# Hybrid attention and RWKV-7 block on one core: the state's decay on GpSimd, its sum on VectorE, and the group norm of 512 tokens before the scan's end

## The chip, the core and the metric

The kernel runs on one core of one Trainium2 chip, as one launch. The metric is the device time of that launch in microseconds. The engines are named as the profile names them: PE is TensorE (PEld its weight loads), DVE is VectorE, ACT is ScalarE, POOL is GpSimd, SP is SyncE, whose queue issues all DMAs of this kernel.

## The reference

One layer of a diffusion backbone over 2048 latent tokens of width 1024, with 256 context tokens ahead of them. All data are fp32. The latent tokens go through an RMS norm, one wide projection, two mixer branches, a merge, and a squared-ReLU MLP. Branch A is windowed attention. Branch B is an RWKV-7 scan in both directions, 8 heads of 64 channels:

```python
def step(S, inp):
    r_t, w_t, kk_t, b_t, k_t, v_t = inp
    sa = jnp.einsum('bhvk,bhk->bhv', S, -kk_t)
    S = S * w_t[:, :, None, :] + sa[..., None] * b_t[:, :, None, :] + v_t[..., None] * k_t[:, :, None, :]
    y = jnp.einsum('bhvk,bhk->bhv', S, r_t) if emit else None
...
mu = jnp.mean(y, axis=-1, keepdims=True)
var = jnp.mean(jnp.square(y - mu), axis=-1, keepdims=True)
yn = (y - mu) * lax.rsqrt(var + LNX_EPS)
...
out = (yn.reshape(B, L, RWKV_WIDTH) * lnx_w + lnx_b + bonus.reshape(B, L, RWKV_WIDTH)).astype(hg.dtype)
g = jax.nn.sigmoid(hg) @ gate_g2
return out * g
...
x = x + gate1 * ((ga * (ya @ w_branch_attn) + gr * (yr @ w_branch_rwkv)) @ w_out)
x = x + gate2 * (jnp.square(jax.nn.relu(h @ w_up)) @ w_down)
out = rmsnorm(x, norm_f_g)
```

## The kernel before

The program has four stages. The first (to about 982 us) projects the tokens, computes the second branch's inputs and leaves them in DRAM: `ka_d`, `rho_d`, `v_d`, and `bk_d`, which holds b and k per chunk of 64 tokens. The second runs the scan, and beside it, to fill PE, the attention, sixteen groups of gate projections and the attention branch's projection. The third merges the branches. The fourth is the MLP.

**The scan.** There are 36 steps, each one chunk of 64 tokens in each of the two directions, four chunks to a window, nine windows. The state of a direction lies as `w[r, 1, h]` in the step's tile `w`, 64 x 256 for each half `r` of the partitions. A step has six parts. Part 0 is `chain_g`: state times keys on PE (`ch<-w,kr`), copied by ACT to `g`. Part 1 is `chain_u`: `g` times the chunk's inverse `st` (`ch<-g,st`), copied by ACT into `w`. Part 2 is `chain_s`: PE adds up the new state in PSUM, first the old state through a product with the identity (`ch<-w,ident`, fp32), then b and k, transposed in `bt`, times the chunk's vectors (`ch<-w,bt`); DVE multiplies the sum by the chunk's decay `pc` and writes it as the next step's state (L710). Then follow the chunk's outputs (`ch<-bm,w`, `ch<-kr,w`). Part 3 is `turn`: PE transposes the next step's `bks` (`tb`), ACT copies it to `bt`. Parts 4 and 5 are `before`: the next step's products of b, k with keys and receptances (`gb`), masked by DVE.

**The inverse.** For each window of four steps, ahead of its use, DVE works out the inverses of the chunks' triangular matrices, in an unbroken row of small operations in SBUF (L588, L590) with transposes around them (L582, L599).

**What runs beside.** After each part, `beside` advances the attention (`attend`) twice and the filler (`fill`) once: gate projections of the first 1024 tokens (`gate`, `gt<-gh,gw_hi`; weights split by ACT into `gw_hi` and by POOL into `gw_lo`), then the attention branch of four blocks of 512 tokens (`branch`, `gt<-ya_h,wa_h`, one PSUM bank, read by DVE at L991). The last block needs the last attention output `ya_d`. `mods` loads the remaining modulation weights (`adp<-ada_w,silr`), one piece a step.

**The order on each engine** is not that of the source alone: the tile framework orders each engine's instructions by its own plan of when operands come; only the scan's matmuls (`rpe`) keep their order among themselves. Each engine then runs its list strictly in order.

**The merge.** `rwkv_out(tb)` does the group norm, the bonus and the gate of 512 tokens; the blocks come as 1, 0, 2, 3. `load_branch` brings `w_branch_rwkv`. `merge_weights` makes `gate1` and `gate2` as rows along all partitions (16 products with diagonal tiles `dg`), scales `w_out` by gate1 and splits it into `wo_h`, `wo_l`; it stands after the first block's branch products (`mb`) and before its output products (`mm`).

Of the kernel before, what the change touches and what calls it, by code (L numbers as in the profile page):

```python
# [22 lines left out]
H = 8  # L23
# [24 lines left out]
def tile_hybrid_block(ctx: ExitStack, tc: tile.TileContext, io: dict, out: bass.AP):  # L48
# [15 lines left out]
    ma_d = dram.tile([KC, P, SEQ], F32, name="ma_d")  # L64
    bon_d = dram.tile([NP, P, SEQ], F32, name="bon_d")
# [20 lines left out]
    def col(o, n=1):  # L86
        return pp[:, o:o + n]
# [953 lines left out]

    att, flr = attend(), fill()
# [13 lines left out]

    mods = (x for m in range(4) for x in ada2(m))
# [10 lines left out]
    for i, _ in enumerate(first):  # L1068
        if i == 0:
            for s in cur:  # L1070
                turn(s)
        if 1 <= i < 3:
            before(cur[i - 1])
# [25 lines left out]
    for _ in att:  # L1099
        pass  # L1100
    for _ in flr:
        pass
# [11 lines left out]
    p3 = ExitStack()  # L1114
    mo = p3.enter_context(tc.tile_pool(name="mo", bufs=1, reuse_waits="tile"))
    mw = p3.enter_context(tc.tile_pool(name="mw", bufs=1, reuse_waits="tile"))
    mb = p3.enter_context(tc.tile_pool(name="mb", bufs=2, reuse_waits="tile"))
    mp = p3.enter_context(tc.tile_pool(name="mp", bufs=2, reuse_waits="tile"))
# [20 lines left out]
    def rwkv_out(tb):  # L1139

        t0 = tb * TB
        yT = mp.tile([P, NP, TB], F32, name="yT", bufs=1)
# [56 lines left out]
    wo_h = mo.tile([P, KC, D], F32R, name="wo_h")  # L1199
    wo_l = mo.tile([P, KC, D], F32R, name="wo_l")  # L1200

    def merge_weights():
# [4 lines left out]
        for m, half, dst in ((0, 0.5, gate1), (3, 1.0, (gate2[:, 0:512], gate2[:, 512:D]))):  # L1207
# [8 lines left out]

        w_out = io["w_out"].rearrange("(k p) n -> p k n", p=P)
        for k in range(KC):
# [5 lines left out]
            act.activation(wo_h[:, k], raw, AF.Copy)  # L1224
            (pool, dve)[k % 2].tensor_tensor(out=wo_l[:, k], in0=raw, in1=wo_h[:, k].bitcast(F32), op=ALU.subtract)

    blocks = (1, 0, 2, 3)
    br = rwkv_out(blocks[0])
    for at, tb in enumerate(blocks):
# [16 lines left out]
        if at == 0:  # L1246
            merge_weights()
        if at + 1 < len(blocks):
            br = rwkv_out(blocks[at + 1])
        for i in range(TB // P):  # L1250
            x = mw.tile([P, D], F32, name="x1t", bufs=2)
            sp.dma_start(out=x, in_=io["x"][t0 + i * P:t0 + (i + 1) * P])
            for hf in range(2):
                cs = slice(hf * 512, (hf + 1) * 512)
                ps = mps.tile([P, 512], F32, name="mm")
                for k in range(KC):
                    lh, ll = mh[:, k, i * P:(i + 1) * P], ml[:, k, i * P:(i + 1) * P]
                    pe.matmul(ps, lh, wo_h[:, k, cs], start=(k == 0), stop=False)  # L1258
                    pe.matmul(ps, lh, wo_l[:, k, cs], start=False, stop=False)  # L1259
                    pe.matmul(ps, ll, wo_h[:, k, cs], start=False, stop=(k == KC - 1))  # L1260
# [228 lines left out]
```

## Time and profile before

| what | value |
|---|---|
| median of 3 runs | 4223.32 us (4220.43 to 4228.75) |
| the profiled execution's own time | 4228.56 us |
| its span, first to last instruction | 4226.8 us |
| TensorE busy | 3865.3 us, 91% of the span |
| VectorE busy | 2171.9 us, 51% |
| ScalarE busy | 1359.5 us, 32% |
| GpSimd busy | 1349.6 us, 32% |
| mean granted TensorE clock | 0.932 of full speed |
| DMA engines busy in the MLP, from 2800 us on | 0.20 of their time |

The shares are means over four stages that have different limits. A clock of 1.0 is 2.4 GHz, 0.5 is 1.2 GHz; a mean between them says what part of a stretch ran at which. A wait counts only where the engine that sets the pace waits.

### The profile page before, as it was taken

What the parts mean: (1) busy time and instruction counts of PE and PEld (TensorE: products, weight loads), DVE (VectorE), ACT (ScalarE), POOL (GpSimd) and SP (SyncE); (2) the same over time, 40 slices, a digit from 0 to 9 for tenths busy, and PEclk for the clock granted to TensorE, in tenths of its full rate; (3) what the DMA queues carried; (4) which work ended last, traced back from release to release, by engine and by line L of the source; (5) the groups of instructions that cost most, each with busy time, mean ns of one, the idle gap of its engine ahead of it and who ended that gap; (6) DMA issues with size and microseconds to landing.
All of it is one profiled execution on the core that took longest, in us unless ns stands there. A gap on an engine that the chain in (4) does not pass through costs nothing.

```text
span 4226.8 us, 67796 instructions
## 1 busy us (share of the span) xinstructions
PE 3865.3 (91%) x26788; PEld 3148.4 (74%) x26788; DVE 2171.9 (51%) x3794; ACT 1359.5 (32%) x2476; POOL 1349.6 (32%) x1104
## 2 busy tenths in 40 slices
PE   7989978897899989888898779989999999999999
PEld 5778868785677767766676658768888888888887
DVE  3355277767576366556566364444443345444334
ACT  2353444554343333322322233331212213112121
POOL 3353555554221110000000174533433334443231
PEclk8999979897999989797897889999999999999999
DMA  6665566666544445343442545542211214211111
GB/s 236 202 195 158 161 183 188 188 185 184 164 138 138 125 131 148 106 132 96 131 139 83 158 150 179 176 154 65 70 50 40 60 41 130 69 60 60 40 55 45
DMA packets 617587, 529.95 MB, mean 125 GB/s; under 512 B 156212, under 2 KB 536340, under 8 KB 616244
## 3 DMA queue, kind: packets, MB, share of 16 engines
q1 hardware_dynamic: 617268, 525.60, 41.6%
q8 instruction: 211, 3.46, 0.3%
q14 instruction: 108, 0.88, 0.1%
HBM read 381.09 MB, written 144.38 MB: 124 GB/s over the span
## 4 chain that ended last, share of the span: by engine, by line
PE 58%; DVE 6%; DMA 4%; issue 2%; POOL 2%; SPq 1%; ACT 1%; POOLq 0%; DVEq 0%; ACTq 0%
PE fd L1343 5%; PE fd L1344 5%; PE fd L1345 5%; PE fu L235 5%; PE fu L236 5%; PE fu L237 5%; PE ch L535 5%; PE gt L947 3%; PE ops L883 3%; PE gb L535 2%; DVE au L582 1%; PE sc L835 1%; PE mm L1260 1%; PE mm L1258 1%; PE mm L1259 1%
## 5 line engine op out<-in xcount | busy, mean ns | idle before, releaser
L235 PE MATMUL acc<-hh,w_hi 128*128 128x384 f32 (+6 forms) x1304 | 457.4, 353 | 41.6 <-ACT hh L211 18.9
L237 PE MATMUL acc<-hh,w_lo 128*128 128x384 f32 (+6 forms) x1304 | 455.8, 351 | 10.3 <-POOL w_lo L229 10.3
L236 PE MATMUL acc<-hl,w_hi 128*128 128x384 f32 (+6 forms) x1304 | 456.5, 351 | 4.8 <-POOL hl L212 4.8
L1349 DVE TENSOR_TENSOR acc<-fd,acc 128x512 f32<-128x512 f32 x480 | 322.3, 686 | 249.1 <-PE fd L1345 246.8
L235 PE MATMUL fu<-h2h,up_h 128*128 128x512 f32 x1024 | 403.4, 394 | 5.8 <-ACT rl L1330 5.8
L1343 PE MATMUL fd<-dn_h,g_h 128*128 128x512 f32 x1024 | 399.8, 390 | 3.5 <-DVE acc L1347 3.5
L236 PE MATMUL fu<-h2l,up_h 128*128 128x512 f32 x1024 | 402.6, 393 | 0.0
L237 PE MATMUL fu<-h2h,up_l 128*128 128x512 f32 x1024 | 402.0, 393 | 0.0
L1333 DVE TENSOR_TENSOR g_l<-rl,g_h 128x512 fp32r<-128x512 f32 x128 | 150.0, 1173 | 487.4 <-POOL rl L1332 487.4
L1344 PE MATMUL fd<-dn_l,g_h 128*128 128x512 f32 x1024 | 399.7, 390 | 0.0
L1345 PE MATMUL fd<-dn_h,g_l 128*128 128x512 f32 x1024 | 398.3, 390 | 0.0
L235 PEld LDWEIGHTS acc<-hh,w_hi 128*128 128x128 f32 (+2 forms) x1304 | 256.1, 197 | 67.1 <-ACT hh L211 21.8
L1332 POOL TENSOR_TENSOR rl<-rl 128x512 f32<-128x512 f32 x128 | 149.9, 1171 | 469.2 <-ACT g_h L1331 469.1
L229 POOL TENSOR_TENSOR w_lo<-w_raw,w_hi 128x1024 fp32r<-128x1024 f32 (+1 forms) x92 | 232.7, 2532 | 205.9 <-ACT w_hi L228 185.7
L1330 ACT ACTIVATE rl<-fu 128x512 f32<-128x512 f32 x128 | 76.2, 597 | 654.1 <-PE fu L237 644.9
L237 PEld LDWEIGHTS acc<-hh,w_lo 128*128 128x128 f32 (+2 forms) x1304 | 255.7, 196 | 31.4 <-POOL w_lo L229 12.5
L236 PEld LDWEIGHTS acc<-hl,w_hi 128*128 128x128 f32 (+2 forms) x1304 | 256.0, 196 | 25.1 <-POOL hl L212 6.0
L1287 POOL TENSOR_TENSOR dn_l<-raw,dn_h 128x1024 fp32r<-128x1024 f32 x64 | 155.6, 2450 | 275.1 <-ACT dn_h L1286 275.1
L845 DVE TENSOR_REDUCE mm<-sc 128x1 f32<-128x256 f32 (+1 forms) x256 | 119.0, 477 | 237.9 <-PE sc L837 152.2
L235 PEld LDWEIGHTS fu<-h2h,up_h 128*128 128x128 f32 x1024 | 193.1, 189 | 49.3 <-ACT rl L1330 6.0
L1343 PEld LDWEIGHTS fd<-dn_h,g_h 128*128 128x128 f32 x1024 | 192.9, 188 | 44.9 <-DVE acc L1347 4.0
L237 PEld LDWEIGHTS fu<-h2h,up_l 128*128 128x128 f32 x1024 | 192.7, 188 | 43.5
(305 smaller groups left out, 8292.3 us busy)
## 6 DMA issues: line engine op xcount, KB each, us to landing
w_raw<-in_w_in SPq DMA_DIRECT2D x74, 512.0 KB
raw<-in_w_mlp_up SPq DMA_DIRECT2D x64, 512.0 KB
raw<-in_w_mlp_down SPq DMA_DIRECT2D x64, 512.0 KB
bk_d<-bk SPq DMA_DIRECT2D x36, 512.0 KB
w<-v_d SPq DMA_DIRECT2D x144, 128.0 KB
gw_raw<-in_w_in SPq DMA_DIRECT2D x32, 512.0 KB
ada_w<-in_w_ada SPq DMA_DIRECT2D x32, 512.0 KB
gt<-g_d SPq DMA_DIRECT2D x64, 256.0 KB
```

The source lines that it names most:

```text
L229: pool.tensor_tensor(out=lo[:, :, :m], in0=raw[:, :, :m], in1=hi[:, :, :m].bitcast(F32), op=ALU.subtract)
L235: pe.matmul(ps[:m, :n], wh[:, k, :m], hh[:, k, :], start=(k == 0), stop=False)
L236: pe.matmul(ps[:m, :n], wh[:, k, :m], hl[:, k, :], start=False, stop=False)
L237: pe.matmul(ps[:m, :n], wl[:, k, :m], hh[:, k, :], start=False, stop=(k == KC - 1))
L535: return self.link(nc.tensor.matmul(*a, **k))
L1287: eng.tensor_tensor(out=lo, in0=raw, in1=hi.bitcast(F32), op=ALU.subtract)
L1332: pool.tensor_tensor(out=rl, in0=rl, in1=rl, op=ALU.mult)
L1333: dve.tensor_tensor(out=glo[:, j], in0=rl, in1=gh[:, j].bitcast(F32), op=ALU.subtract)
L1343: pe.matmul(ps, lh, dn[j][0][:, cs], start=(j == 0), stop=False)
L1344: pe.matmul(ps, lh, dn[j][1][:, cs], start=False, stop=False)
L1345: pe.matmul(ps, ll, dn[j][0][:, cs], start=False, stop=(j == FG - 1))
L1349: dve.tensor_tensor(out=acc[:, cs], in0=ps, in1=acc[:, cs], op=ALU.add)
```

## The change

Four edits, and the order of some parts.

1. The state is decayed by POOL, ahead of time: after `chain_g` of a step POOL writes `nxt.w[r, 1, h] = s.w[r, 1, h] * pc` (four operations of 64 x 256 a step). The identity product goes. The sum in PSUM holds only the b, k product, and DVE adds it to what POOL wrote.
2. For this b and k must carry the decay too: the new `decay(s)` multiplies `bks` (128 x 512) by `pc` on POOL, after `before` has read it and before `turn` transposes it. So `before` moves to parts 3 and 4 and `turn` to part 5.
3. `early` does the group norm, bonus and gate of tokens 512 to 1023 in the last window, in quarters of 128 tokens, and stores the result in `yw_d`; the merge's first block then only loads and splits it.
4. `merge_weights` stands before the first block's branch products; its gate2 part comes last; `wo_h`, `wo_l` become one tile per eighth, half of them in a pool of their own, and the pool `mp` comes first in its stage. `mods` goes ahead by one or two pieces a step.

```diff
+    def decay(s):
+
+        pool.tensor_tensor(out=s.bk, in0=s.bk, in1=pc[:, s.d, :, s.c:s.c + 1].broadcast_to([P, NP, P]), op=ALU.mult)
...
-            for s in pair:
-                for h, r in enumerate(hh):
-                    rpe.matmul(s.cp[r, 0], ident[r, r], s.w[r, 1, h], start=True, stop=False, skip_group_check=True)
             for s, nxt in zip(pair, nxts):
                 for p in range(NP):
                     for h, r in enumerate(hh):
-                        rpe.matmul(s.cp[r, 0, p], s.bt[:, p, r], s.w[:, 0, h, p], start=False, stop=True,
+                        rpe.matmul(s.cp[r, 0, p], s.bt[:, p, r], s.w[:, 0, h, p], start=True, stop=True,
                                   skip_group_check=True)
                 for h, r in enumerate(hh):
-                    dve.tensor_tensor(out=nxt.w[r, 1, h], in0=s.cp[r, 0],
-                                      in1=pc[r, s.d, :, s.c:s.c + 1].broadcast_to([C, NP, C]), op=ALU.mult)
+                    dve.tensor_tensor(out=nxt.w[r, 1, h], in0=s.cp[r, 0], in1=nxt.w[r, 1, h], op=ALU.add)
...
+    def early():
...
+        for i in range(EBN // P):
...
+            ps = bank(atp, "ey", "at")
+            for p in range(NP):
+                pe.transpose(ps[:, p * P:(p + 1) * P], yT[:, p], ident)
...
+            pool.tensor_tensor(out=s1[:, 1], in0=s1[:, 1], in1=expo[:, :H], op=ALU.pow)
+            pool.tensor_tensor(out=y3c, in0=y3c, in1=s1[:, 1].unsqueeze(2).broadcast_to([P, H, C]), op=ALU.mult)
+            yield
...
+            dve.tensor_tensor(out=yw, in0=gp.rearrange("p (a t) -> p a t", a=NP), in1=yw, op=ALU.mult)
+            sp.dma_start(out=yw_d[:, :, i * P:(i + 1) * P].rearrange("a p t -> p a t"), in_=yw)
...
-                    next(mods, None)
+                    for s, nxt in zip(cur, nxts):
+                        if nxt is not None:
+                            for h, r in enumerate(hh):
+                                pool.tensor_tensor(out=nxt.w[r, 1, h], in0=s.w[r, 1, h],
+                                                   in1=pc[r, s.d, :, s.c:s.c + 1].broadcast_to([C, NP, C]), op=ALU.mult)
+                    for _ in range(1 + step % 2):
+                        next(mods, None)
...
-                elif part == 3 and nxts[0] is not None:
+                elif part < 5 and nxts[0] is not None:
+                    before(nxts[part - 3])
+                    decay(nxts[part - 3])
+                elif part == 5 and nxts[0] is not None:
                     for s in nxts:
                         turn(s)
-                elif part > 3 and nxts[0] is not None:
-                    before(nxts[part - 4])
                 next(ahead_of, None)
+                if w == NWIN - 1:
+                    ey = ey or early()
+                    for _ in range(2 - part % 2):
+                        next(ey, None)
                 beside(TICKS)
...
+        if EB0 <= t0 < EB0 + EBN:
...
+            for p in range(NP):
+                yw = mp.tile([P, TB], F32, name="yw")
+                sp.dma_start(out=yw, in_=yw_d[p, :, t0 - EB0:t0 - EB0 + TB])
+                split(yh[:, p], yl[:, p], yw)
+            return yh, yl
...
     br = rwkv_out(blocks[0])
+    merge_weights()
...
-        if at == 0:
-            merge_weights()
```

How the instructions stand now, at three places. First PE in step 33 of the scan, from the product with the inverse to the chunk's outputs; the two numbered `ch` tiles are the two directions. Before:

```order
L535 MATMUL ch_23656<-g,st 64x64 x8
L535 MATMUL ch_23667<-g,st 64x64 x8
L535 MATMUL ch_23656<-w,ident 64x256 x2
L535 MATMUL ch_23667<-w,ident 64x256 x2
L535 MATMUL ch_23656<-w,bt 64x64 x8
L535 MATMUL ch_23667<-w,bt 64x64 x8
L535 MATMUL ch_23656<-bm,w 64x64 x8
```

The same place of the change:

```order
L538 MATMUL ch_23857<-g,st 64x64 x8
L538 MATMUL ch_23868<-g,st 64x64 x8
L538 MATMUL ch_23857<-w,bt 64x64 x8
L538 MATMUL ch_23868<-w,bt 64x64 x8
L538 MATMUL ch_23857<-bm,w 64x64 x8
```

The four identity products of the step are gone, and nothing has come in their place.

Then PE at the end of the scan, around the last two rows of the last step's outputs (`ch<-bm,w`, `ch<-kr,w`); `gt<-ya...` is the last block of the attention branch, `ops` and `ot` the attention itself. Before:

```order
L990 MATMUL gt<-ya_h,wa_l 128x512
L535 MATMUL ch_24122<-bm,w 64x64 x8
L535 MATMUL ch_24111<-kr,w 64x64 x8
L535 MATMUL ch_24122<-kr,w 64x64 x8
L988 MATMUL gt<-ya_h,wa_h 128x512
L989 MATMUL gt<-ya_l,wa_h 128x512
L990 MATMUL gt<-ya_h,wa_l 128x512
```

The same place of the change:

```order
L886 MATMUL ops<-vtok,pT 128x65 x4
L538 MATMUL ch_24330<-bm,w 64x64 x3
L538 MATMUL ch_24341<-bm,w 64x64 x8
L538 MATMUL ch_24330<-kr,w 64x64 x8
L538 MATMUL ch_24341<-kr,w 64x64 x8
L899 MATMUL ot<-ident,on 128x128 x4
L1291 MATMUL mt<-dg,ones 128x128 x8
L991 MATMUL gt<-ya_h,wa_h 128x512
L992 MATMUL gt<-ya_l,wa_h 128x512
L993 MATMUL gt<-ya_h,wa_l 128x512
```

Before, the last attention block ended with step 32, and the 96 products of the branch's last block stood between and behind the chain's last steps. Now the attention's last products stand between the chain's last steps, and all 96 branch products follow the scan in one row, with the first `mb` right behind them.

Last POOL late in the scan, where it had only memsets (`st`, `pack`) and the branch's splits (`ya_l`) to do. Before:

```order
L595 MEMSET st 32x32x32 x2
L826 MEMSET pack 128x64 x2
L595 MEMSET st 32x32x32 x2
L826 MEMSET pack 128x64
L979 TENSOR_TENSOR ya_l<-raw,ya_h 128x512 x4
```

The same stretch of the change:

```order
L1143 TENSOR_TENSOR w<-w,pc 64x256 x4
L664 TENSOR_TENSOR bks<-bks,pc 128x512 x2
L829 MEMSET pack 128x64
L598 MEMSET st 32x32x32 x2
L1143 TENSOR_TENSOR w<-w,pc 64x256 x2
L664 TENSOR_TENSOR bks<-bks,pc 128x512
L1143 TENSOR_TENSOR w<-w,pc 64x256 x2
L664 TENSOR_TENSOR bks<-bks,pc 128x512
```

Each step now has four decays of the state (`w`) and two of b and k (`bks`) in POOL's list.

## Rows read from the trace of the kernel before

**Rows 1.** Page, part 1: busy time, share of the span, instructions.

```profile
PE 3865.3 (91%) x26788; PEld 3148.4 (74%) x26788; DVE 2171.9 (51%) x3794; ACT 1359.5 (32%) x2476; POOL 1349.6 (32%) x1104
```

**Rows 2.** Stretches: length; busy of PE, PEld, DVE, ACT, POOL; clock, DMA share, GB/s.

```profile
1124.00:1526.00 402.00, 385.31 (x4146) 299.32 (x4144) 225.96 (x486) 149.10 (x276) 66.68 (x40) 0.98 0.47 131
1526.00:1880.00 354.00, 311.21 (x3966) 246.96 (x3964) 204.30 (x429) 118.70 (x232) 26.55 (x26) 0.87 0.45 132
1880.00:2344.00 464.00, 402.44 (x5120) 318.85 (x5116) 272.36 (x609) 138.72 (x271) 9.71 (x12) 0.86 0.39 113
2344.00:2420.00 76.00, 61.05 (x645) 45.83 (x641) 19.98 (x46) 13.05 (x28) 7.95 (x8) 0.87 0.55 164
2420.00:2475.00 55.00, 40.72 (x173) 28.21 (x172) 31.97 (x55) 15.43 (x25) 40.45 (x35) 0.88 0.50 148
2475.00:2520.00 45.00, 31.67 (x90) 19.13 (x91) 36.44 (x39) 17.06 (x22) 36.92 (x24) 0.66 0.57 169
2520.00:2800.00 280.00, 271.13 (x1223) 215.56 (x1223) 126.82 (x197) 93.10 (x167) 129.16 (x123) 0.98 0.54 175
2800.00:4226.80 1426.80, 1404.47 (x6126) 1152.22 (x6124) 605.19 (x740) 314.37 (x432) 509.44 (x302) 0.99 0.20 63
```

**Rows 3.** Groups by line: busy us, mean ns of one, idle before.

```profile
L535 PE MATMUL ch<-w,ident 64*64 64x256 f32 x280 | 49.0, 440 | 11.9 <-ACT w L695 11.5
L710 DVE TENSOR_TENSOR w<-ch,pc 64x256 f32<-64x256 f32 x140 | 58.9, 421 | 51.2 <-PE ch L535 38.0 <-issue 6.8 <-ACT pT L880 2.4
```

**Rows 4.** PE in order of time in one step, clock full: start, length us.

```profile
2301.72 1.08 PE L535 MATMUL ch<-w,ident 64*64 64x256 f32 x8
2302.73 0.80 PE L535 MATMUL ch<-w,bt 128*64 128x64 f32 x18
```

**Rows 5.** PE's waits, 1124 to 2345 us: us in total, times, longest.

```profile
PE sT L873 <- DVE mm L845: 26.3, 11, 5.9
PE sc L835 <- DVE qA L815: 11.9, 3, 6.1
```

**Rows 6.** Two lines of POOL: ns of one, min/median/max.

```profile
L1161 POOL TENSOR_TENSOR yc<-yc,s x16: 1031/1044/1544, 2421.6 to 2658.1; 128x512 f32<-128x512 f32 x16
L463 POOL TENSOR_TENSOR ks<-ks,ta x32: 721/901/4893, 343.9 to 1052.8; 128x256 f32<-128x256 f32 x32
```

**Rows 7.** DVE and POOL in order of time, during an inverse.

```profile
1353.35 2.62 POOL L929 TENSOR_TENSOR gw_lo<-gw_raw,gw_hi 128x1024 fp32r<-128x1024 f32 x1 [0.88 <-ACT gw_hi L928]
1353.75 2.46 DVE L590 TENSOR_TENSOR tn<-tn,itmp 128x220 f32<-128x220 f32 x1
```

**Rows 8.** Groups by line: the inverse's row on DVE, all nine windows.

```profile
L590 DVE TENSOR_TENSOR tn<-tn,itmp 128x31 f32<-128x31 f32 (+15 forms) x279 | 106.9, 383 | 6.5
L588 DVE TENSOR_TENSOR itmp<-tn,au 128x31 f32<-128x31 f32 (+15 forms) x279 | 97.9, 351 | 6.9
```

**Rows 9.** PE in order of time at the scan's end; [idle before it].

```profile
2342.57 0.66 PE L896 MATMUL ot<-ident,on 128*128 128x128 f32 x4
...
2351.81 1.09 PE L538 MATMUL tb<-ident,bks 128*128 128x128 f32 x8
2357.34 0.68 PE L988 MATMUL gt<-ya_h,wa_h 128*128 128x512 f32 x1 [4.43 <-ACT ya_h L978]
...
2401.72 0.50 PE L988 MATMUL gt<-ya_h,wa_h 128*128 128x512 f32 x1 [0.89 <-DVE gt L991]
...
2410.44 0.79 PE L988 MATMUL gt<-ya_h,wa_h 128*128 128x512 f32 x1 [5.67 <-DVE gt L991]
```

**Rows 10.** The chain of waits from 2340 to 2540 us: start, length.

```profile
2405.50 3.74 DMA yo<-y_d
...
2419.66 0.69 DVE gt L991
...
2439.05 0.70 PE mb L1240 x2
...
2501.99 3.47 DVE x1t L1223 x2
...
2506.59 0.79 PE mm L1258
```

More of the change, by code (lines that the diff above doesn't have):

```diff
@@ L1040, in fill, with load @@
             yield from branch(brp, raw_of, wa, t)
+    def early():
+        wk = [ip.tile([P, 4, NP, P], F32, name="yw0", tag="ga", bufs=1), ip.tile([P, 4, NP, P], F32, name="yw1", tag="st")]
+        aw = ip.tile([P, 1024], F32, name="g2e", tag="au", bufs=1)
+        sg = ip.tile([P, 2, P], F32, name="sge", tag="itmp", bufs=1)
+        g2 = aw[0:96, 0:512]
+        sp.dma_start(out=g2, in_=io["gate_g2"])
+        def load(i):
+            t0 = EB0 + i * P
+            for j in range(P // C):
+                sp.dma_start(out=wk[i % 2][:, 0, :, j * C:(j + 1) * C], in_=y_d[t0 // C + j])
+            sp.dma_start(out=sg[0:96, i % 2], in_=sg_d[:, t0:t0 + P])
+            sp.dma_start(out=wk[i % 2][:, 3], in_=bon_d[:, :, t0:t0 + P].rearrange("a p t -> p a t"))
+        load(0)
+        for i in range(EBN // P):
+            yT, yc, yw, bt = (wk[i % 2][:, j] for j in range(4))
+            s1 = aw[:, 512 + i % 2 * 2 * H:512 + (i % 2 + 1) * 2 * H].rearrange("p (b h) -> p b h", h=H)
+            if i + 1 < EBN // P:
+                load(i + 1)
+            ps = bank(atp, "ey", "at")
+            for p in range(NP):
+                pe.transpose(ps[:, p * P:(p + 1) * P], yT[:, p], ident)
+            y3 = ps.rearrange("p (h c) -> p h c", c=C)
+            dve.tensor_reduce(out=s1[:, 0], in_=y3, axis=AX.X, op=ALU.add)
+            dve.tensor_scalar(out=s1[:, 0], in0=s1[:, 0], scalar1=-1.0 / C, scalar2=None, op0=ALU.mult)
+            ycf = yc.rearrange("p a b -> p (a b)")
+            y3c = ycf.rearrange("p (h c) -> p h c", c=C)
+            dve.tensor_tensor(out=y3c, in0=y3, in1=s1[:, 0].unsqueeze(2).broadcast_to([P, H, C]), op=ALU.add)
+            act.activation(yw, yc, AF.Square)
+            dve.tensor_reduce(out=s1[:, 1], in_=yw.rearrange("p a b -> p (a b)").rearrange("p (h c) -> p h c", c=C),
+                              axis=AX.X, op=ALU.add)
+            pool.tensor_scalar(out=s1[:, 1], in0=s1[:, 1], scalar1=1.0 / C, scalar2=1e-5 * C, op0=ALU.mult, op1=ALU.add)
+            pool.tensor_tensor(out=s1[:, 1], in0=s1[:, 1], in1=expo[:, :H], op=ALU.pow)
+            pool.tensor_tensor(out=y3c, in0=y3c, in1=s1[:, 1].unsqueeze(2).broadcast_to([P, H, C]), op=ALU.mult)
+            yield
+            ps = bank(atp, "eb", "at")
+            for p in range(NP):
+                pe.transpose(ps[:, p * P:(p + 1) * P], yc[:, p], ident)
+            for p in range(NP):
+                act.activation(yw[:, p], ps[:, p * P:(p + 1) * P], AF.Identity, scale=col(O_LW + p), bias=col(O_LB + p))
+            pool.tensor_tensor(out=yw, in0=yw, in1=bt, op=ALU.add)
+            yield
+            gp = bank(atp, "eg", "at")
+            for p in range(NP):
+                pe.matmul(gp[:, p * P:(p + 1) * P], g2[:, p * P:(p + 1) * P], sg[0:96, i % 2], start=True, stop=True)
+            dve.tensor_tensor(out=yw, in0=gp.rearrange("p (a t) -> p a t", a=NP), in1=yw, op=ALU.mult)
+            sp.dma_start(out=yw_d[:, :, i * P:(i + 1) * P].rearrange("a p t -> p a t"), in_=yw)
+            yield
@@ L1068, in tile_hybrid_block @@
     for i, _ in enumerate(first):
-        if i == 0:
+        if i < 2:
+            before(cur[i])
+            decay(cur[i])
+        elif i == 2:
             for s in cur:
                 turn(s)
-        if 1 <= i < 3:
-            before(cur[i - 1])
         beside(1)
@@ L1098, in tile_hybrid_block @@
             pass
[L1099 to L1102, printed above, removed]
+    for it in (ey, att, flr):
+        for _ in it:
+            pass
     p2.close()
@@ L1197, in second_norm @@
             sp.dma_start(out=h2_d[i, :, kh * 4:kh * 4 + 4], in_=hf)
-    wo_h = mo.tile([P, KC, D], F32R, name="wo_h")
-    wo_l = mo.tile([P, KC, D], F32R, name="wo_l")
+    wo_h = [(mv if k < KC // 2 else mo).tile([P, D], F32R, name=f"wo_h{k}") for k in range(KC)]
+    wo_l = [(mv if k < KC // 2 else mo).tile([P, D], F32R, name=f"wo_l{k}") for k in range(KC)]
     def merge_weights():
@@ L1206, in merge_weights, with along @@
         gate1 = [mw.tile([P, 512], F32, name="gate1", tag="wt", bufs=2) for hf in range(2)]
-        for m, half, dst in ((0, 0.5, gate1), (3, 1.0, (gate2[:, 0:512], gate2[:, 512:D]))):
+        def along(m, half, dst):
             for hf in range(2):
```

21 lines of the change are left out of this document (15 added, 6 removed).

## The prediction

> **What bounds the kernel now.** I read the page's busy shares first. PE is busy for 91% of the span, DVE for 51%, ACT and POOL for 32% each [rows 1]. So the question at each place is whether PE itself sets the pace or waits.
>
> The stretches answer it by stage [rows 2]. The MLP from 2800 us on keeps PE busy for 1404.47 of 1426.8 us at a clock of 0.99; the change doesn't touch it. In the scan, from 1124 to 2344 us, PE is busy for 385.31 + 311.21 + 402.44 = 1099 of 1220 us, which is 90%. The 121 us without work are short waits of several kinds, most of them on DVE; the two largest sums are 26.3 and 11.9 us, both of the attention [rows 5]. No wait on the chain of states stands among these two. So the scan is mostly paced by the number of matmuls in PE's list, and the reader should see that work taken off PE there is worth about its own time.
>
> The seam between scan and merge is different. From 2344 to 2520 us PE has idle 14.95 + 14.28 + 13.33 = 42.6 us, and its clock is 0.87, 0.88 and 0.66 [rows 2]. A mean clock of 0.66 says that 68% of the stretch ran at 1.2 GHz; over the three stretches that is 19.8 + 13.2 + 30.6 = 63.6 us at half rate, which costs up to 31.8 us if PE had work all the while. Idle and half rate together leave 74 us there to be had at most. The chain of waits names the causes: a branch product that waits 5.67 us for DVE [rows 9], which stands behind a 3.74 us load of earlier outputs, then the group norm, from the last branch result at 2419.66 us to the first steady `mb` at 2439.05 us, then the scaled eighths of `w_out`, which the first `mm` meets only at 2506.59 us [rows 10].
>
> **The change, part by part.**
>
> *Identity product.* It is 280 PE instructions, busy for 49.0 us [rows 3]. A step's eight take from 2301.72 to 2302.73 us, 1.01 us at full clock [rows 4]; 35 steps of that are 35 us, and the rest of the 49 is half clock. In its place nothing comes on PE. PE was busy for 90% of the scan, so I take 90% of 49.0, which is 44 us. The bounds are 0 (all of it becomes idle time) and 49.
>
> *DVE's part.* It stays one operation of 64 x 256 from PSUM with one operand from SBUF, 421 ns [rows 3]: no change, with ACT's copies unchanged too. It now also waits for POOL.
>
> *POOL's part.* No row shows these two shapes. A product of 128 x 512 with a broadcast factor takes 1.04 us [rows 6], which I take as 1.05 for `bks`. For 64 x 256, half of that is 0.52; the row of 128 x 256 has a median of 0.90. I take 0.55, since time goes by elements for each partition. So a step adds 4 x 0.55 + 2 x 1.05 = 4.3 us to POOL, and the scan 140 x 0.55 + 72 x 1.05 = 153 us; the bounds are 140 x 0.52 + 72 x 1.03 = 147 and 140 x 0.90 + 72 x 1.54 = 237. POOL was busy for 66.68 + 26.55 + 9.71 = 103 of these 1220 us [rows 2], so it has room. The decay of the state needs only what the step before left, and the sum that reads it comes after two PE products and two ACT copies; a step takes some 35 us (1220 us over the 33 to 34 steps in it). What hides it is this slack. Its risk is what stands ahead of it in POOL's list: the splits `gw_lo`, which wait for `gw_hi`. In the new lists every state decay has no more splits ahead of it than the same step's ACT copies have `gw_hi` ahead of them, so ACT is held up by the same weights already. I take nothing for it.
>
> *POOL against DVE.* This is the cost that I do charge. While POOL held a split of 2.62 us from 1353.35 us, a 128 x 220 sum of the inverse, begun at 1353.75, took 2.46 us, until POOL was done [rows 7]; the mean of its line is 383 ns [rows 8]. So operations of DVE that read two tiles of SBUF stand still while POOL works. The Trainium skill says so too (SBUF — State Buffer, section on rules for kernel authors): a vector operation with two SBUF inputs and a GpSimd operation that reads SBUF exclude each other, the second blocks fully. By that rule alone all of POOL's added time could be lost to DVE. By the trace, such work of the inverse is 106.9 + 97.9 = 205 us [rows 8], in and a little ahead of the scan's 1296 us, about 16% of it, so 16% of 153 us, 24 us, meets it; and DVE waits, not PE, which has other work. I take 10 us lost, between 0 and 24.
>
> *Order of the step.* `turn` comes right behind `before`, with the decay between them on POOL: `gb`, 1.05 us, `tb`. `bt` is wanted only two parts into the next step, and other matmuls stand between in PE's list. I take 0; without that cover it is 1.05 us a step, 37 us, inside the first rival. `mods` moves 12 steps' products forward and adds none.
>
> Scan: 44 - 10 = **34 us gained**, between -24 and 49.
>
> *The seam.* Gone: the wait of 5.67 us, since no branch product stands ahead of the last outputs any more; the idle time of the group norm, which I put at 10 of the 14.28 us [rows 2]; about 7 us of half clock in that stretch (13.2 / 2); and in 2475 to 2520 most of 13.33 us idle and 15 us half clock, of which I take 20, since `w_out` is now loaded under the branch's last block. That is 43 us. Added: the last attention output has to be stored, loaded and split before the branch can start. This took from 2342.57 + 0.66 = 2343.2 to 2357.34 us, 14.1 us, of which the chain's step hid all but 4.43 [rows 9]. In the new list only eight small products stand there, so about 10 us more come to light. The branch's eight rounds run with one bank and nothing between them: seven times 0.89 us [rows 9], 6 us. And the group norm's PE work (32 transposes and 16 gate products; eight `tb` instructions, four transposes, take 1.09 us [rows 9], so near 9 us, and 3 for the gates) goes to the last window, where a third of it may fill idle time; the stretch that it leaves had counted it as busy, so it is only a loss of cover, 3 us. Sum: 43 - 10 - 6 - 3 = **24 us gained**. The bounds are 55 (74 less the 19 us added) and -19 (nothing of the waits goes, and the added ones come).
>
> Sum: 34 + 24 = 58 us. The profiled execution took 4228.6 us (its span is 4226.8), so 4170.6 against its own time; it lies 5.2 us above the median of the runs, 4223.3, so in medians **4165 us**.
>
> **Rivals.** *PE is not the pace in the scan.* The removed products only lengthen waits, and idle PE then runs at half rate, as from 1526 us on, where the clock is 0.86 to 0.87 [rows 2]. For it speaks that idle time there is 104 of 818 us; against it, that PE is busy for 96% up to 1526. Only the seam is left: 4223 - 24 = 4199.
>
> *The seam gives nothing.* The uncovered start of the branch, POOL's splits of `w_out` ahead of the branch's own `ya_l`, and loads that crowd SP take back what the norm and the weights give: 4223 - 34 = 4189.
>
> *More than forecast.* With shorter chain steps the short waits shrink too, and the seam reaches its bound: 4223 - 49 - 55 = 4119.
>
> *Slower.* POOL's decays come onto the path: the inverse on DVE waits for POOL, POOL for DVE, and the chain's sum for both. Its price is up to 153 us, and it outweighs 44 + 24 = 68 us of gain from 68 / 153 = 44% on. At 60% the time is 4223 - 68 + 92 = 4247. For it speaks the blocked sum of rows 7; against it the 16% above, and the sum itself, which takes one operand from PSUM. The Trainium skill's page on the GpSimd engine (GPSIMD Engine Reference, section Engine selection) advises against such products there, about twice VectorE's time for two inputs; no row compares the two here on this shape, and POOL's free time makes it a matter of place, not of speed.
>
> **How the numbers follow.** Forecast, within 20 us of 4165: 0.48. Scan gives nothing: 0.17. Seam gives nothing: 0.13. More: 0.14. Slower: 0.08. The range for 8 in 10 runs from 4112, just past the fast rival, to 4210, past the weak scan. 0.2% of this time is 8.4 us, about what a measurement can tell from no change. All cases but the slow one are faster by more than that; I move 0.04 of them to "same" or beyond, since the weak cases can come together: faster 0.88, same 0.05, slower 0.07.
>
> **What would show it.** Right: no `ch<-w,ident` on PE; the scan's last `ch<-kr,w` some 20 us or more earlier than before; POOL's `w<-w` near 0.55 and `bks` near 1.05 us; the first `mb` right behind the last branch product; the stretch to the first `mm` at a higher clock. Wrong: PE waits for the DVE sum with POOL as its releaser; the inverse's lines with means well above 351 and 383 ns; PE as idle in the scan as before plus 40 us; or a gap of 20 us and more between `ot` and the first branch product.

## The result, and the profile after

The changed kernel takes 4204.61 us (median of 6 runs, 4201.89 to 4209.21) against 4225.91 of before in the same runs: a ratio of 0.9950, with a 95% interval of 0.9938 to 0.9963. It is faster by 21 us, inside the forecast's range and with its sign, but by little more than a third of the 58 us forecast. Its profiled execution has a span of 4200.1 us, which is 26.7 less than before.

The page's first part, to be laid beside [rows 1]:

```profile
PE 3809.9 (91%) x26473; PEld 3130.3 (75%) x26532; DVE 2197.9 (52%) x3794; ACT 1362.6 (32%) x2488; POOL 1506.7 (36%) x1316
```

PE has 55 us less work in the whole span, and its share is the same 91%. POOL has 157 us more, and DVE, which was given no new work in the scan, has 26 us more.

The stretches of [rows 2] in the changed kernel; the seventh ends where the MLP's last 1426.8 us begin:

```profile
1124.00:1526.00 402.00, 374.47 (x4024) 294.99 (x4038) 231.95 (x478) 142.59 (x265) 113.33 (x99) 0.97 0.49 138
1526.00:1880.00 354.00, 302.54 (x3929) 243.31 (x3948) 216.04 (x450) 122.68 (x238) 71.02 (x81) 0.88 0.47 138
1880.00:2344.00 464.00, 395.94 (x5308) 324.46 (x5327) 295.86 (x636) 149.38 (x296) 92.01 (x114) 0.88 0.42 118
2344.00:2420.00 76.00, 49.15 (x303) 37.01 (x304) 28.40 (x46) 17.75 (x31) 25.24 (x19) 0.71 0.57 168
2420.00:2475.00 55.00, 46.19 (x204) 35.69 (x203) 33.01 (x45) 14.98 (x22) 30.58 (x21) 0.98 0.58 183
2475.00:2520.00 45.00, 45.00 (x207) 35.43 (x206) 17.82 (x33) 15.39 (x29) 22.40 (x25) 0.98 0.46 150
2520.00:2773.30 253.30, 230.82 (x1033) 181.07 (x1031) 106.96 (x176) 80.46 (x147) 119.80 (x112) 0.96 0.51 162
2773.30:4200.10 1426.80, 1408.12 (x6149) 1155.50 (x6148) 618.61 (x740) 318.94 (x433) 507.51 (x302) 0.99 0.21 65
```

In the scan's 1220 us PE is busy for 374.47 + 302.54 + 395.94 = 1073 us, where it was 1099: the missing product has become idle time there (147 us for 121). From 2420 to 2520 the forecast came true: PE idles 8.8 us where it idled 27.6, at a clock of 0.98 where it was 0.88 and 0.66. Two stretches lost what that gained. From 2344 to 2420 PE idles 26.9 us at a clock of 0.71 (before 15.0 at 0.87), and in the stretch up to the MLP it idles 22.5 us (before 8.9).

The groups of the moved work and of the inverse, for [rows 3, 6, 8]:

```profile
L593 DVE TENSOR_TENSOR tn<-tn,itmp 128x31 f32<-128x31 f32 (+15 forms) x279 | 115.8, 415 | 6.0
L591 DVE TENSOR_TENSOR itmp<-tn,au 128x31 f32<-128x31 f32 (+15 forms) x279 | 113.9, 408 | 6.8
L1143 POOL TENSOR_TENSOR w<-w,pc 64x256 f32<-64x256 f32 x140 | 91.9, 656 | 354.7 <-PE ch L538 294.8 <-DVE w L714 23.8 <-DVE mm L848 17.4
L664 POOL TENSOR_TENSOR bks<-bks,pc 128x512 f32<-128x512 f32 x72 | 77.9, 1082 | 174.7 <-PE gb L538 105.5 <-issue 47.8 <-DMA kr<-ka_d 9.1
L714 DVE TENSOR_TENSOR w<-ch,w 64x256 f32<-64x256 f32 x140 | 58.9, 421 | 31.2 <-PE ch L538 13.1 <-ACT w L702 7.7 <-DMA qraw<-q_d 4.6
```

POOL's decays take 91.9 + 77.9 = 169.8 us (forecast 153), and the sum on DVE its old 421 ns. The inverse has the same 558 operations but takes 229.7 us where it took 204.8 [rows 8]. One of its operations under a decay, DVE and POOL in order of time, as in [rows 7]:

```profile
1513.25 0.73 DVE L593 TENSOR_TENSOR tn<-tn,itmp 128x255 f32<-128x255 f32 x1
1514.01 0.73 DVE L591 TENSOR_TENSOR itmp<-tn,au 128x256 f32<-128x256 f32 x1
1514.53 1.11 POOL L664 TENSOR_TENSOR bks<-bks,pc 128x512 f32<-128x512 f32 x1
1514.77 1.15 DVE L593 TENSOR_TENSOR tn<-tn,itmp 128x256 f32<-128x256 f32 x1
```

The sum begun at 1514.77 ends only when POOL is done, 0.28 us behind it, and takes 1.15 us where its neighbours of the same size take 0.73. The Trainium skill (SBUF — State Buffer, section on rules for kernel authors) says that of a DVE operation with two SBUF inputs and a GpSimd operation that reads SBUF the second to issue blocks until the first is done; this trace agrees.

PE at the end of the scan, for [rows 9]:

```profile
2361.76 1.11 PE L886 MATMUL ops<-vtok,pT 128*128 128x65 f32 x8
2362.80 0.91 PE L538 MATMUL ch<-bm,w 128*64 128x64 f32 x22
2363.64 1.15 PE L538 MATMUL ch<-kr,w 64*64 64x64 f32 x32
2364.72 0.66 PE L899 MATMUL ot<-ident,on 128*128 128x128 f32 x4
2368.31 3.18 PE L1291 MATMUL mt<-dg,ones 128*128 128x128 f32 x10 [2.94 <-DVE dg L1289]
...
2377.73 0.79 PE L991 MATMUL gt<-ya_h,wa_h 128*128 128x512 f32 x1 [2.35 <-ACT ya_h L981]
...
2390.43 0.79 PE L991 MATMUL gt<-ya_h,wa_h 128*128 128x512 f32 x1 [8.85 <-ACT ya_h L981]
...
2429.12 0.40 PE L1320 MATMUL mb<-yr_h,br_hi 128*128 128x512 f32 x1
```

The chain ends at 2364.8, 36 us earlier than before (2400.9). But the attention ends with it, at 2365.4, where it had ended at 2343.2 [rows 9], and all of the branch's last block comes behind. The first branch product stands 12 us behind the end of `ot`, and another waits 8.85 us. So the branch ends at 2429.3, which is 10 us later than before (2419.6), and `mb` follows at once.

PE at the seam between merge and MLP (`fu` is the MLP's first product), and the chain of waits there:

```profile
2760.88 0.39 PE L1338 MATMUL mm<-wo_h,m_l 128*128 128x512 f32 x1
2761.11 0.60 PE L1266 MATMUL mt<-ident,x1t 128*128 128x128 f32 x4
2768.40 1.11 PE L1266 MATMUL mt<-ident,x1t 128*128 128x128 f32 x4 [6.70 <-ACT h2f L1270]
...
2782.47 1.22 PE L238 MATMUL fu<-h2h,up_h 128*128 128x512 f32 x2 [3.10 <-ACT h2h L1364]
```

```profile
2758.04 0.25 PE mm L1337
2758.30 6.23 DMA raw<-in_w_mlp_up
2764.62 1.06 ACT up_h L1364
```

The last `mm` ends at 2761.3, 36 us earlier than before (2797.5), yet `fu` begins at 2782.5, 8 us later than before (2774.5): the MLP's first weights are loaded only when a late `mm` has been read. This place is not in the forecast at all.

### The profile page after: what moved, and what is told of

Same layout as the page of the kernel before. It is cut to its first block, busy times and chain, and to the rows that moved or that the text cites. A ratio compares the mean times of both kernels' runs of the same rounds, so it can differ in the third digit from the quotient of the medians.

```text
span 4200.1 us, 67810 instructions
## 1 busy us (share of the span) xinstructions
PE 3809.9 (91%) x26473; PEld 3130.3 (75%) x26532; DVE 2197.9 (52%) x3794; ACT 1362.6 (32%) x2488; POOL 1506.7 (36%) x1316
## 5 line engine op out<-in xcount | busy, mean ns | idle before, releaser
L1411 DVE TENSOR_TENSOR g_l<-rl,g_h 128x512 fp32r<-128x512 f32 x128 | 158.8, 1241 | 482.6 <-POOL rl L1410 482.6
L239 PEld LDWEIGHTS fu<-h2l,up_h 128*128 128x128 f32 x1024 | 192.8, 188 | 43.5 <-DVE h2l L1365 0.8
```

What stands on the lines that cost most here:

```text
L239: pe.matmul(ps[:m, :n], wh[:, k, :m], hl[:, k, :], start=False, stop=False)
L1411: dve.tensor_tensor(out=glo[:, j], in0=rl, in1=gh[:, j].bitcast(F32), op=ALU.subtract)
```

## The experiments

All ratios are to the kernel before in the same runs, with 95% intervals of 0.13% to 0.32% to each side, which is 5 to 13 us; the interval of a difference is worked out from the two (root of the sum of squares), and "by the ratios" is the difference of two ratios times 4225 us. "Order" is the new order of the parts alone. Steps are counted from 0, and a step begins with its first copy of `g`.

| run | median, us | ratio (95%) |
|---|---|---|
| e1 no identity product | 4189.94 | 0.9920 (0.9898 to 0.9941) |
| e2 scan edits alone | 4211.57 | 0.9967 (0.9951 to 0.9982) |
| e3 the rest alone | 4200.31 | 0.9944 (0.9919 to 0.9969) |
| e4 change, `mp` last | 4188.40 | 0.9917 (0.9887 to 0.9947) |
| e6 change, `mods` one a step | 4207.62 | 0.9962 (0.9949 to 0.9975) |
| e8 change, decays twice | 4263.20 | 1.0090 (1.0064 to 1.0116) |
| e9 change, `mp` last, `mods` one | 4206.34 | 0.9961 (0.9942 to 0.9981) |
| e10 order | 4190.63 | 0.9915 (0.9883 to 0.9946) |
| e12 order, no identity product | 4191.49 | 0.9931 (0.9905 to 0.9957) |
| e14 order, POOL's decays unread | 4218.48 | 0.9989 (0.9976 to 1.0003) |
| e11 change, decays on ACT | 4221.46 | 0.9995 (0.9981 to 1.0008) |
| e13 order and rest, `mp` last | 4199.12 | 0.9948 (0.9928 to 0.9967) |
| e17 change, half the inverse | 4167.91 | 0.9878 (0.9851 to 0.9906) |
| e18 e12, half the inverse | 4166.39 | 0.9863 (0.9841 to 0.9885) |
| e15 change, one `graw` | 4228.72 | 1.0019 (1.0004 to 1.0033) |
| e16 order, merge weights | 4184.26 | 0.9905 (0.9882 to 0.9929) |
| e19 e9 without the early norm | 4199.98 | 0.9927 (0.9901 to 0.9954) |
| e20 e13 without the early norm | 4187.94 | 0.9904 (0.9881 to 0.9928) |

**The two halves.** e1 takes the identity product out of the kernel before, and the old state with it. e2 makes all of the scan's edits there and none of the merge's, e3 the reverse.

```diff
-            for s in pair:
-                for h, r in enumerate(hh):
-                    rpe.matmul(s.cp[r, 0], ident[r, r], s.w[r, 1, h], start=True, stop=False, ...)
```

> The kernel before without the identity product and with nothing in its place, so the old state is left out of each sum. First theory (PE paces the scan, and the change's own additions took the gain back): 44 us below before, about 4182 us. Second theory (up to 1860 us the scan is paced by waits, so that taken PE time turns into idle time): 10 to 25 us below, about 4205 us, with step 20 starting at 1880 us or later as before (1889 us).

> The scan's edits alone (decay on POOL, sum on DVE, order of the parts), one piece of modulation weights a step, merge as before. If POOL's operations and the later turn cost what the product gave: 15 to 25 us slower than the run without the identity product. If they are hidden: within 5 us of it.

> The early group norm, the merge's new order and pools and the faster modulation weights, with the identity product kept. First theory (the seam gives its 24 us): about 4201 us. Second theory (the gain at the merge's start is lost again where the MLP starts): within 8 us of before, 4218 to 4234 us, with the MLP's first matmul later than the merge's last one by 15 us or more.

The product alone is worth 35 us, the scan's edits together only 13, the rest 24. So the decay, or the order that it needs, takes some 22 us back; and 13 + 24 = 37 is more than the change's 21, so the halves share something or hurt each other. The traces show what they share. Steps 20 to 31, columns as in [rows 2], first of the kernel before and then of e3:

```profile
1889.40:2319.30 429.90, 368.34 (x4708) 291.62 (x4709) 259.07 (x574) 126.34 (x246) 9.71 (x12) 0.85 0.39 113
```

```profile
1895.50:2300.90 405.40, 356.98 (x4639) 287.16 (x4661) 258.21 (x567) 126.00 (x246) 9.58 (x12) 0.86 0.40 114
```

e3 has the old scan but for `mods`, and yet these steps take 405 us where they took 430. Its traced execution is 32 us shorter than that of before: the last step begins 24 us earlier (2366.8 for 2390.5), and all that follows is 8 us shorter. So most of e3's gain lies in the scan and not in the seam. The same steps take 403 us in e2 and 404 in the change: these 25 us can be had once. Which of e3's edits brings them no run shows.

**The order alone** (e10, on the kernel before):

```diff
-                elif part == 3 and nxts[0] is not None:
+                elif part < 5 and nxts[0] is not None:
+                    before(nxts[part - 3])
+                elif part == 5 and nxts[0] is not None:
                     for s in nxts:
                         turn(s)
-                elif part > 3 and nxts[0] is not None:
-                    before(nxts[part - 4])
```

> The kernel before with only the parts' order of the change: the next step's products of b and k in parts 3 and 4, the turn in part 5; identity product kept, nothing on POOL. First theory (POOL's block is the loss): within 5 us of before, 4220 to 4230 us. Rival (the later turn frees the buffer of b and k late, and the loads queue behind it): 12 to 20 us slower, about 4240 us.

Both theories missed: the order is a gain of 32 us by itself. PE's waits on the chain's products in the scan of the kernel before (us in total, times, longest):

```profile
PE ch L535 <- ACT w L695: 10.7, 6, 6.3
PE ch L535 <- DVE kr L676: 9.8, 3, 5.6
PE ch L535 <- DVE w L710: 8.3, 1, 8.3
```

The second line is the first product of a step waiting for its masked keys, which DVE writes between the operations of the inverse's row. With `before` a part earlier in the step no such wait is left in e10's list, and the other two are 3.8 and 6.8 us there. Two steps that had one of these waits show what it held up: step 21 took 37.1 us at a clock of 0.72 and takes 20.2 at 1.00, step 25 took 39.2 at 0.74 and takes 29.6 at 0.83.

**Do the two gains add up?** e12 is e10 without the identity product (the old state left out); e14 is e10 with POOL's decays written where DVE and ACT overwrite them unread, so that PE keeps its product.

```diff
+        for h, r in enumerate(hh):
+            pool.tensor_tensor(out=s.w[r, 0, h], in0=s.bk[r, :, h * C:(h + 1) * C], in1=pc[...], op=ALU.mult)
...
+                                pool.tensor_tensor(out=nxt.w[r, 1, h], in0=s.w[r, 1, h], in1=pc[...], op=ALU.mult)
```

> The kernel before with the parts in the new order and without the identity product; the old state is left out of the sum, nothing is decayed on POOL, the merge is as before. Theory A (POOL's decays eat the gain): the order alone gave 34 us and the missing product alone 35, each is a gain of its own, so together about 4225 - 65 = 4160, and the 36 steps end some 80 us earlier than before. Theory B (both gains are the same one: steps after the tenth have a floor that PE does not set): about 4185 to 4192, and the 36 steps end 45 us earlier, as with either alone.

> The kernel before with the parts in the new order, the identity product kept, and POOL given the decays of every step as in the change (eight operations of 64x256 a step), but into places that DVE and ACT overwrite before anything reads them; so POOL's work and the wait for it are there and PE loses nothing. Theory A: POOL's 170 us cost what the sum of the parts lacks, 45 to 55 us over the order alone, so 4235 to 4245. Theory B: POOL's work costs at most the 10 us of the forecast, so 4190 to 4202.

They don't add up: e12 has e10's time. From step 20 to step 32, stretch and columns as in [rows 2], first e10 and then e12:

```profile
1883.50:2285.10 401.60, 358.12 (x4742) 285.98 (x4740) 259.39 (x577) 129.69 (x252) 9.67 (x12) 0.89 0.43 123
```

```profile
1888.40:2288.50 400.10, 349.21 (x4636) 281.44 (x4635) 259.43 (x577) 128.84 (x251) 10.30 (x12) 0.87 0.43 122
```

PE does 9 us less in e12, and the twelve steps last the same 400 us; in e1 they take 406. Over steps 0 to 31 PE is busy for 1072 us and idle for 121 in the kernel before, at a clock of 0.90. In e1 it is busy for 1018 and idle for 133 (0.92), in e10 busy for 1055 and idle for 103 (0.93), and in e12 busy for 1034 and idle for 126 (0.91). So on top of the order the missing product comes back as idle time and as a lower clock. PE's waits in steps 20 to 31 of e12:

```profile
PE yp L535 <- DVE t L603: 8.9, 2, 7.2
PE tb L538 <- DVE bm L678: 7.7, 6, 5.6
PE sT L870 <- DVE mm L842: 6.6, 3, 3.5
PE ch L535 <- DVE w L707: 5.1, 3, 4.2
PE sc L832 <- DVE mm L842: 5.1, 2, 4.9
```

All of the longest are waits for DVE. e14 lies between its two forecasts, 28 us above e10, with an interval of some 15 us to each side. The inverse, first in e10 and then in e14:

```profile
L588 DVE TENSOR_TENSOR itmp<-tn,au 128x31 f32<-128x31 f32 (+15 forms) x279 | 106.8, 383 | 6.3
L590 DVE TENSOR_TENSOR tn<-tn,itmp 128x31 f32<-128x31 f32 (+15 forms) x279 | 100.8, 361 | 6.6
```

```profile
L590 DVE TENSOR_TENSOR tn<-tn,itmp 128x31 f32<-128x31 f32 (+15 forms) x279 | 118.5, 425 | 6.6
L588 DVE TENSOR_TENSOR itmp<-tn,au 128x31 f32<-128x31 f32 (+15 forms) x279 | 113.8, 408 | 6.3
```

That is 207.6 and 232.3 us: DVE's row takes 24.7 us longer beside 183 us of decays, about what the kernel lost. The change's own decays can be priced too: e2 has them and e12 does not, and e2 gains 18 us less (15 by the ratios, with some 13 to each side).

**What sets the floor?** e17 leaves half of the inverse's row out of the change, e18 out of e12.

```diff
+            if k % 2:
                 dve.tensor_tensor(out=t, in0=tn[:, k:, k:k + 1]..., in1=au[:, k:k + 1, 0:k]..., op=ALU.mult)
                 dve.tensor_tensor(out=tn[:, k:, 0:k], in0=tn[:, k:, 0:k], in1=t, op=ALU.add)
```

> The changed kernel with every second step of the inverse's row on DVE left out (half of its 558 operations), so the inverse is not the true one. Theory D (DVE's list paces the scan from the tenth step on, so work taken off PE only becomes idle PE, and what POOL takes from DVE is lost in full): about 115 us leave DVE, and the 36 steps end 25 to 60 us earlier, 4145 to 4180. Theory L (the steps are paced by the latency of their own chain, DVE's load is beside it): within 8 us of the changed kernel, 4197 to 4213.

> The kernel before with the new order and no identity product (the old state left out, nothing decayed on POOL), and half of the inverse's row on DVE left out as well. Theory D: the missing product at last shows its worth, 25 us or more below the same kernel with the whole inverse, 4145 to 4168. Theory L: the same floor, 4183 to 4195.

Both times lie where the theory put them that DVE's list is the pace: 37 us less than the change and 25 less than e12 (30 and 29 by the ratios), with PE's products untouched. But e17 took 111 us off the row and e18 95, so a third or less came back: the row is part of the pace and not all of it. Steps 20 to 31 of e18:

```profile
1866.60:2250.50 383.90, 330.53 (x4604) 270.68 (x4625) 233.25 (x487) 127.22 (x248) 9.75 (x12) 0.92 0.45 128
```

DVE has 26 us less, and the stretch is 16 us shorter. PE does not idle less (53.4 us for 50.9 in e12): its busy time is 19 us shorter, with nearly the same number of products, at a clock of 0.92 for 0.87. One of its waits is 4 us or longer; in e12 four are.

**How much does POOL cost?** e8 issues every decay a second time into a tile that nobody reads; for its room it gave up one buffer of the raw gate weights, `graw`, and e15 is the change with that edit alone. e11 gives the decays to ACT, 24 operations a step.

```diff
+        pool.tensor_tensor(out=junk, in0=junk, in1=pc[...], op=ALU.mult)
-            raw = gap.tile([P, GBL], F32, name="graw", bufs=2)
+            raw = gap.tile([P, GBL], F32, name="graw", bufs=1)
```

> The change with every decay on POOL issued a second time into a tile that nobody reads, 170 us more of POOL; the staging tile of the gate's inputs has one buffer in place of two, to make room. First theory (POOL blocks DVE's operations on two SBUF tiles, and that is what the scan lost): the inverse's 558 operations take 15 to 25 us longer in sum than 230 us, and the kernel 15 to 25 us longer than the change, about 4224 us. Rival (POOL is hidden, the loss is that of the later turn): within 5 us of the change.

> The changed kernel with one buffer instead of two for the raw gate weights, nothing else. The doubled decays had this edit too. If their 58 us were POOL's, this stays within 8 us of the changed kernel, 4197 to 4213; if they came from the gate weights' loads in the first ten steps, 4225 to 4250.

> The changed kernel with ACT in POOL's place for the decays (64x64 and 128x128 at a time, 24 operations a step). ACT and DVE do not block each other in any row so far. Theory A: what POOL cost comes back, less what 24 ACT operations a step add ahead of the copies of the chain: 4165 to 4185. Theory B: POOL was no cost, ACT's added work lies before the chain's copies: 4205 to 4230.

e8 is slower than either of its forecasts. Of its 58 us, 24 are the buffer's and 34 are left for the second dose (30 by the ratios, with some 13 to each side); its inverse takes 256.7 us where e15's takes 233.5. These decays hung on nothing, and most ran in the first ten steps, so the dose isn't the first one again; but 28 in e14 and 34 here are of one size. In e11 the inverse takes 212.8 us, as without decays on POOL (e1 212.2), and yet the gain is gone: ACT's decays alone are 247 us of work in the list of the engine that copies `g`, `u` and `bt` for the chain. So the block on DVE is a price of POOL, but ACT does not do the work free either.

**The seams.** e4 puts the pool `mp` last again in the merge's stage; e6 loads `mods` one piece a step; e9 does both.

```diff
-    mp = p3.enter_context(tc.tile_pool(name="mp", bufs=2, reuse_waits="tile"))
     mo = p3.enter_context(tc.tile_pool(name="mo", bufs=1, reuse_waits="tile"))
...
     mv = p3.enter_context(tc.tile_pool(name="mv", bufs=1, reuse_waits="tile"))
+    mp = p3.enter_context(tc.tile_pool(name="mp", bufs=2, reuse_waits="tile"))
```

```diff
-                    for _ in range(1 + step % 2):
-                        next(mods, None)
+                    next(mods, None)
```

> The change with the pool mp put last again in the merge's stage. First theory (in the change the MLP's first weights lie where the merge's output weights are read until its last product, and so their loads wait for it): the loads start before the merge ends, the idle time of about 20 us at the MLP's start goes, about 4185 us. Rival (the loads wait for the SP queue and the DMAs anyway): within 5 us of the change, 4200 to 4210 us.

> The change with one piece of modulation weights a step, as before. Theory (the faster pieces share one buffer with the attention's queries and hold the attention back, so that it ends with the scan and the branch's last block runs uncovered): the attention's last product ends 15 us or more before the chain's, the uncovered stretch shrinks, about 10 us below the change, 4195 us. Rival (the attention lags because the chain got faster): within 5 us of the change.

> The change with mp last in the merge's stage and one piece of modulation weights a step. If both losses are separate: 16 + 10 us below the change, about 4178 us. If the second is no loss: 4188 us as with mp last alone.

In e4 the MLP begins under the merge; PE in order of time:

```profile
2746.82 0.39 PE L1338 MATMUL mm<-wo_h,m_l 128*128 128x512 f32 x1
2747.05 0.62 PE L238 MATMUL fu<-h2h,up_h 128*128 128x512 f32 x2
2747.51 0.39 PE L1336 MATMUL mm<-wo_h,m_h 128*128 128x512 f32 x1
```

From the last `mm` to the end the change takes 1438.8 us and e4 1410.9. But the merge now starts 9 us after the branch and not at once, and 16 us are left of the 28. In e9 the MLP's part is as short (1411.0), the merge still longer, and the sum equals e6's, above both of e9's forecasts. So the pool's place moves a wait from one seam to the other; it is worth between 0 and 16 us. `mods` is worth nothing that shows beside `mp` first (e6), and the late attention is not its doing: in e6 it also ends only with the chain. With `mp` last the faster `mods` is 18 us ahead (e4 against e9, some 15 to each side); why, no run shows.

**The early norm.** e13 is e10 with the rest of the change and `mp` last, so all but the moved decay. e20 is e13 and e19 is e9, each with the early norm taken out and that block's norm back in the merge. e16 is e20 with `mods` one a step.

```diff
-                if w == NWIN - 1:
-                    ey = ey or early()
-                    for _ in range(2 - part % 2):
-                        next(ey, None)
```

> All of the change but the moved decay: the identity product and DVE's product are kept, the new order, the early norm and the merge's order are in, and the pool mp stands last in its stage. Theory A and B both: order 34, rest 24, pool 16, less what of the rest's gain lay in the scan and is the same as the order's (up to 26): 4150 to 4177. If the late attention takes the order's gain, about 4184.

> The kernel before with the new order of the parts and, of the rest, the merge weights ahead of the first block's branch products, their tiles by eighths and gate2 last; no early norm, no decays on POOL, identity product kept. If the order's gain (34 us) and that of the weights in the seam are apart: 4170 to 4185. If the norm's idle time before the first block hides the weights anyway: within 6 us of the order alone, 4185 to 4196.

> The changed kernel without the early norm (the first block's norm is again in the merge), with mods one a step and the pool mp last. The same kernel with the early norm took 4206. Theory N (the early norm holds up the last attention block by as much as it saves in the merge, or more): 4185 to 4206. Theory M (the early norm is worth the 10 us and more of the forecast): 4212 to 4225.

> As the order with the merge weights (4184), but mods one or two a step as in the change; it is also the kernel of order and rest (4199) without its early norm. Theory N: the early norm was the difference between those two, 4178 to 4192. If mods were the difference: 4193 to 4206.

e13 came out above all of its forecasts. Without the early norm both kernels are faster, in ratio by 0.0034 and 0.0044, with some 0.0033 and 0.0031 to each side, so each is just clear of noise. PE at the scan's end in e19:

```profile
2338.91 0.55 PE L899 MATMUL ot<-ident,on 128*128 128x128 f32 x3
...
2389.16 1.15 PE L538 MATMUL ch<-kr,w 64*64 64x64 f32 x32
```

The attention ends 51 us ahead of the chain, as before, and the branch's last block lies between the chain's steps again. With the early norm in the last window (e9), 56 of the last 64 `ops` products stood in steps 33 to 35; without it (e19) none does. The norm takes the attention's PSUM banks (`at`) and adds work to every engine there; which of the two holds the attention up is not shown.

e16 and e20 are the fastest kernels here that compute the whole: the new order and the merge weights ahead, the identity product kept, nothing decayed on POOL, no early norm. At 0.9905 and 0.9904 their intervals end at 0.9929 and 0.9928, below that of the changed kernel, which begins at 0.9938. From e10 (0.9915), and from e4 (0.9917), which has the decays and the early norm, they can't be told.

## Why the prediction came out wrong in size

**The scan, 34 us forecast, 13 by itself (e2).** The forecast was 44 for the product less 10 for POOL. Measured, product and order together give 32 (e12), and the decays on POOL take 18 (e2 against e12).
- *Identity product, 44 us.* It is 35 alone (e1), but 0 within some 17 us on top of the order (e10 and e12). The step that failed is "the scan is mostly paced by the number of matmuls in PE's list": in the order that the change needs, that number could fall without the time following. The step rested on PE's busy share of 90%. From 1526 us on, that share is taken at a clock of 0.86 to 0.87 [rows 2], so part of the busy time is slow work between waits. The 121 us of waits, "most of them on DVE", were the sign. The prediction looked at the two largest groups, both of the attention; the three groups of the chain's `ch` come to 10.7 + 9.8 + 8.3 = 28.8 us, more than either. e17 and e18 show that the inverse's row on DVE is part of the pace.
- *Order, 0.* Alone it gives 32 us (e10). I looked only at what `turn` loses by coming later, not at what `before` gains by coming earlier, though DVE's masks stand among the inverse's operations. With the product already gone it adds nothing that shows (e1 and e12), so the change could have about one of the two gains, not both.
- *POOL against DVE, 10 us in 0 to 24.* It is 18 by e2 and e12 and 28 by e14, with 24.7 us more in the inverse. The count of what meets the lock (16% of POOL's time, 24 us) was right; the step that failed is "DVE waits, not PE, which has other work": the kernel lost about as much as the row did. That the block is the whole price is not shown, since e17 took 111 us off the same row and got back 37. The sign named for this case came: the row's means rose from 351 and 383 ns to 408 and 415.

POOL's own time was forecast well enough (656 and 1082 ns for 550 and 1050), and the sum on DVE exactly. That the chain ends 36 us earlier, much as forecast, proves nothing: the attention ends 22 us later, and the branch's last 96 products, of which 36 had stood before the last step, all come behind the chain.

**The seam, 24 us forecast.** By itself (e3) it is 24, but that is luck, a right sum with wrong parts: by e3's trace most of it lies in steps 20 to 31. The changed kernel begins its last step 35 us earlier than before, and what follows takes 9 us more (1845.0 for 1836.3). Of the parts, the waits between `mb` and the `mm` products went as forecast, though one reading was wrong: the first `mm` of the kernel before does not stand at 2506.59 us but at 2475.8 (ns of one, min/median/max, then first and last start in us):

```profile
L1258 PE MATMUL mm<-wo_h,m_h x256: 387/389/796, 2475.8 to 2796.7; 128*128 128x512 f32 x128
```

"About 10 us more" for the uncovered branch was too little: 12 us to its first product, and 8.85 more in front of another. The early norm, put at 10 less 3, is worth nothing or a loss of some 10 (e19, e20): where it stands the attention's last block ends late, a consequence that I did not follow. And the place of `mp`, named in the diff, was given no term; it opened the gap of 21 us in front of the MLP.

**The sum.** 13 and 24 were added up in the forecast's way, as independent; together they are 21. Each by itself shortens steps 20 to 31 by some 25 us, and the two together by 26, which more than covers the 16 that are missing. The rival "PE is not the pace in the scan", at 4199 us, was nearer to the mechanism in the scan, and was given 0.17 where the clock of 0.86 and the many waits on DVE deserved more. That its time is 6 us from the result is luck in part: it put the scan at nothing and the seam at 24, where the scan's edits by themselves gave 13 and what follows the last step became longer.

## What to carry to other kernels

A busy share of 90% does not make an engine the pace: look at its clock in the stretch, add up its short waits by the engine that ends them, and take a little work off that other engine to see whether the time follows. Two edits that shorten the same steps need not add up, so time them together before adding them up, and look at which steps got shorter. Where an edit moves work under another's or changes which pool holds which addresses, follow it to the next seam: here the branch ended 10 us later and the MLP began 8 us later, though the merge's last product came 36 us earlier.

## What was not expected of the hardware

The price of POOL's work on fp32 tiles in SBUF was not POOL's time but DVE's: 170 us of decays lengthened the inverse by 25 us, 183 us of them in e14 by as much, and moving them to ACT brought the inverse back to 212.8 us. How much of a decay's cost is this block and how much the order of the lists around it is not settled beyond the 18 us of e2 against e12 and the 28 us of e14, with some 13 and 15 us to each side.
